# The feed-forward of the latent tokens by seven block products instead of eight, up and down as two phases

## The chip, the core and the metric

The kernel runs on one core of a Trainium2 chip. The metric is the device time of one execution in microseconds (us), as the median of several runs. All data are float32 in DRAM. TensorE gets its dense operands as float32r: each is split into a high part and an exact remainder, and a product costs three passes.

## The reference, cut to what is computed

Two layers share one trunk over 256 context tokens and 1024 latent tokens, with 1024 features. Each layer has a modulated norm, an input projection into four mixers (S5, windowed attention, HGRN2, latent attention), an output projection with a gated residual, and then the part that the change touches, the feed-forward:

```python
def rms_norm(x, g):
    return x * rsqrt(mean(x * x, axis=-1) + EPS) * g
def swiglu(h, w_up, w_down):            # w_up: 1024 x 5632, w_down: 2816 x 1024
    gate, up = split(h @ w_up, 2, axis=-1)
    return (silu(gate) * up) @ w_down
for i in range(2):
    mod = silu_c @ w_mod[i] + b_mod[i]  # 6 * 1024 columns; mod_c likewise for the context
    ...                                 # norm 1, mixers, x = x + g1 * y
    x = x + g2 * swiglu(rms_norm(x, norm2_g[i]) * (1 + sc2) + sh2, ffn_w_up[i], ffn_w_down[i])
    if i == 0:                          # the context as well, with its own modulation
        ctx = ctx + cg2 * swiglu(..., ffn_w_up[i], ffn_w_down[i])
return rms_norm(x, final_norm_g)
```

So the feed-forward of layer 0 covers 1280 tokens and that of layer 1 covers 1024.

## The kernel before

Features lie on the 128 partitions and tokens along them: `x` is a tile of 128 x 8 x 1280. `BLOCKS` cuts the tokens into latent blocks 0 and 1 of 512 and the context block 2 of 256. `H` (class HBuf) holds the scaled input as a high and a low part per block, `Hh` and `Hl`.

**The three passes.** `mm3` (L489 to L494) issues per pair of 128 x 128 weights and a token block three matmuls: high by high, high by low, low by high. `load_split` (L505) loads weights to a staging tile, ScalarE makes the high part (L498) and VectorE, or another engine that is named, the low part (L501).

**The feed-forward.** `ffn` (L1226) goes over the 22 hidden tiles of 128. Per tile it loads two up weights (gate and up, 128 x 8 x 128 each) and one down weight (128 x 1024). `unit_` runs the 24 matmuls of one up product over a token block, then ScalarE's Silu (gate), or VectorE's product with it and a split (up). After two hidden tiles, `down` runs for every block the eight output tiles of these two and adds each to `x` (L1272). So activations never leave SBUF and `x` stays there.

**What runs beside it.** In layer 0 a filler computes layer 1's modulation and S5 matrices. `mod_rows` (L1101) reads a row tile of `w_mod`, and VectorE multiplies it by the condition, once for each of two conditions, with the sum taken on the way (L1116); it yields after each tile, here 96 tiles of 256 KB with two buffers (`modw`), and the condition (`modc`) is loaded per half. Then `s5_build` makes layer 1's matrices in 16 groups; GpSimd (POOL) writes them to DRAM (`s5E`, L312). `paced` (L1727) draws one step of the filler and puts its VectorE work behind what has been traced so far. `ffn` draws a step after each unit and three per block of the down-projection, and what is left before its last tile's end.

**The ends.** `to_next` (L1635) does layer 0's last down-projections block by block: squares, norm 1 of layer 1, loading of the input projection's token weights (`wtmr`, four rounds of 416 KB, then ScalarE and POOL), its first token tiles (`pstm`), then its columns (`psfm`). `to_out` (L1684) does the final norm and the store. The last latent block's norm 2 falls into the first tile of `ffn`, by `start`.

**What sets the order.** The program is traced by a scheduler that gives each engine the ready instruction that stands earliest in the program. A DMA stands in the queue of the engine that issues it (SP's in most cases, POOL's in some) and is held there by its waits. Pools are stacks on the left and the right side of SBUF; a tile that is opened on bytes of an earlier pool waits for that pool's last readers on those bytes.

Of the kernel before, what the change touches and what calls it, by code (L numbers as in the profile page):

```python
# [6 lines left out]
F32 = mybir.dt.float32  # L7
# [9 lines left out]
L = 2  # L17
# [12 lines left out]
# ----------------------------------------------------------------- S5 parameters  # L30
def s5_params(g, raw, keep, big):
    """Powers of a_bar, b_bar, decay and rotation of both layers; layout [(dir, p), layer, group]. raw: lam_re, lam_im, log_dt [128, 3, L * NG]; big: scratch [128, 4096]."""
# [37 lines left out]
    def expm1(x):  # L70
        """(e^x, e^x - 1) to float32 accuracy."""
# [22 lines left out]
    # angle modulo 2 pi, in three parts  # L94
# [27 lines left out]
    # a - 1 without cancellation; b_bar = (a - 1) / lam * B  # L122
# [30 lines left out]
    # powers a^0 .. a^8 : pw[:, re/im, e, (l g)]  # L153
# [10 lines left out]
    # decay over a chunk of 8 and the unit rotation over a chunk  # L164
# [33 lines left out]
def s5_build(g, io, keep, l, gsz, dram, pool, psum, tag):  # L198
# [3 lines left out]
    ls = slice(l * NG, (l + 1) * NG)  # L202
    dsk = g.dsk[:, l]
    # exponents of readout (fwd j+1, bwd 8-j) and drive (fwd 7-j, bwd j)
# [28 lines left out]
    for g0 in range(0, NG, gsz):  # L233
        gs, lg = slice(g0, g0 + gsz), slice(l * NG + g0, l * NG + g0 + gsz)
# [25 lines left out]
        def products(gs=gs, Vm=Vm, R=R, Bz=Bz, Bb=Bb, C=C, nci=nci):  # L260
# [10 lines left out]
            # the products of up to two groups and directions side by side, each on a column tile of its own  # L271
# [19 lines left out]
        # unit rotation e^{i c phi} over the 160 chunks  # L291
# [27 lines left out]
def unit(g, u, ta, tb):  # L319
    """One Newton step to modulus one: u *= 1.5 - 0.5 |u|^2."""  # L320
# [9 lines left out]
def sigmoid(g, out, v, tmp, bias=None):  # L330
    """out = sigmoid(v) by exp and log alone, without overflow."""
# [8 lines left out]
def s5_mixer(g, l, usrc, dram, yraw, last, pool, psum, tag):  # L340
    """usrc: two DRAM [128, T] of the input; yraw: two for the readout. Yields after each part."""
# [107 lines left out]
def s5_glu(g, l, yraw, ydst, blocks, pool, psum, tag):  # L449
    """GELU and GLU of the S5 readout, from DRAM to the high and low parts of the mixers' output. Yields."""  # L450
# [37 lines left out]
def mm3(nc, ps, parts, first=True, last=True):  # L488
    """ps (+)= sum of w^T x over (w_hi, w_lo, x_hi, x_lo) parts, three float32r passes each."""  # L489
    n = len(parts)  # L490
    for i, (wh, wl, xh, xl) in enumerate(parts):
        nc.tensor.matmul(ps, wh, xh, start=first and i == 0, stop=False)  # L492
        nc.tensor.matmul(ps, wh, xl, start=False, stop=False)  # L493
        nc.tensor.matmul(ps, wl, xh, start=False, stop=last and i == n - 1)  # L494
# [9 lines left out]
def load_split(g, pool, shape, src, name, raw, eng=None):  # L504
    """Weights from DRAM as float32r high part and exact remainder; raw: (pool, name) of the staging tile."""  # L505
# [8 lines left out]
# ----------------------------------------------------------------- HGRN2  # L514
# [4 lines left out]
class HGRN:  # L519
    """Gated recurrence of two heads (128 rows) at a time; a token block of one direction after the other, in the order of the scan."""  # L520
# [20 lines left out]
    def unit(self, d, b, z):  # L541
        """z: [128, tn] logits of direction d (PSUM)."""
# [22 lines left out]
        # states and their factors lie value by value; one place more than chunks: the state that enters, whose factor is 0  # L565
# [17 lines left out]
        # keys to token-major, then k^T v of each chunk  # L583
# [14 lines left out]
        # the state leaving a chunk replaces its kv  # L598
# [35 lines left out]
    def finish(self, b, gg, ng, dst):  # L634
        """Head norm and gate gg (PSUM) of one block, to DRAM."""
# [1239 lines left out]
```

## Time and profile before

| | |
|---|---|
| three runs | 3630.08, 3636.73, 3648.10 us; median 3636.73 us |
| the profiled execution: span from first to last instruction | 3633.6 us |
| TensorE (PE) busy | 3460.6 us, 95% |
| VectorE (DVE) busy | 2026.2 us, 56% |
| ScalarE (ACT) busy | 1198.5 us, 33% |
| GpSimd (POOL) busy | 691.0 us, 19% |
| DMA | 280.39 MB, mean 77 GB/s |

Busy times overlap, so they do not add up to the span; an engine that is busy 95% of it has 173 us in which nothing ran on it. PEld is TensorE's loading of weights, which lies beside its matmuls. In rows of the trace, `fpu` is the PSUM bank of an up product, `fpd` of a down product; `out<-in` are names in the program, `x24` is a count, and what stands in brackets is how long the engine had been idle and what it waited for last. One row can stand for several instructions in a row, with their count behind it.

### The profile page before, as it was taken

Reading aid. Unit: us, or ns where it says so; the run is one execution under the profiler, and the core shown is the slowest. Engines: PE = TensorE matmul, PEld = TensorE weight load, DVE = VectorE, ACT = ScalarE, POOL = GpSimd, SP = SyncE. Lnnn points to the kernel's source line nnn. Section 1 sums busy time; section 2 is a strip of 40 time slices with the busy share of each in tenths; the row PEclk is TensorE's granted clock in tenths of the full one; section 3 lists DMA queues with packets and bytes.
Section 4 is the critical chain, followed back from the end, with each engine's and each line's share of the span. In section 5 each row is a group of like instructions: output and inputs, shape, how many; then the busy total and the mean of one; then the engine's idle time right before and its main releaser. Section 6 shows DMA issues by size and latency. Waiting matters only on the chain. (4 is left out here: it accounts for less than half of the span.)

```text
span 3633.6 us, 48522 instructions
## 1 busy us (share of the span) xinstructions
PE 3460.6 (95%) x18654; PEld 2675.0 (74%) x18654; DVE 2026.2 (56%) x4284; ACT 1198.5 (33%) x2120; POOL 691.0 (19%) x1455
## 2 busy tenths in 40 slices
PE   6998998998999999999999998887999999999998
PEld 3877776644678888888888876765644888888887
DVE  7466574568587666555544434564574744334335
ACT  4234444345442111111112435454454521111113
POOL 5730000024320000577100211000045300000000
PEclk8998786899999999999999999786999999999999
DMA  6442213121333333222110332212022311111111
GB/s 207 138 138 95 84 50 99 47 68 40 107 118 112 104 115 105 74 63 59 58 46 18 130 102 88 77 42 58 7 64 71 101 52 47 48 51 47 52 47 58
DMA packets 154503, 280.39 MB, mean 77 GB/s; under 512 B 33344, under 2 KB 81664, under 8 KB 153504
## 3 DMA queue, kind: packets, MB, share of 16 engines
q1 hardware_dynamic: 141120, 260.62, 23.1%
q0 software_dynamic: 3968, 13.77, 1.3%
q10 hardware_dynamic: 9184, 2.91, 0.3%
q8 instruction: 146, 2.39, 0.3%
q14 instruction: 85, 0.70, 0.1%
HBM read 228.14 MB, written 49.09 MB: 76 GB/s over the span
## 5 line engine op out<-in xcount | busy, mean ns | idle before, releaser
L492 PE MATMUL fpu<-Hh,fwh 128*128 128x512 f32 (+1 forms) x1760 | 651.2, 370 | 0.0
L493 PE MATMUL fpu<-Hl,fwh 128*128 128x512 f32 (+1 forms) x1760 | 649.7, 369 | 0.5 <-DVE Hl L1219 0.5
L494 PE MATMUL fpu<-Hh,fwl 128*128 128x512 f32 (+1 forms) x1760 | 648.6, 369 | 0.0
L1272 DVE SCALAR_TENSOR_TENSOR x<-fpd,mod,x 128x512 f32<-128x512 f32 (+1 forms) x448 | 304.9, 686 | 136.6 <-PE fpd L494 134.4
L493 PEld LDWEIGHTS fpu<-Hl,fwh 128*128 128x128 f32 x1760 | 332.2, 189 | 56.8 <-issue 1.2
L492 PEld LDWEIGHTS fpu<-Hh,fwh 128*128 128x128 f32 x1760 | 332.2, 189 | 56.5 <-issue 0.8
L494 PEld LDWEIGHTS fpu<-Hh,fwl 128*128 128x128 f32 x1760 | 332.1, 189 | 56.0 <-DVE fwl L501 0.3
L492 PE MATMUL fpd<-fgh,fdh 128*128 128x512 f32 (+1 forms) x896 | 328.9, 368 | 3.9 <-DVE x L1272 3.3
L493 PE MATMUL fpd<-fgl,fdh 128*128 128x512 f32 (+1 forms) x896 | 327.8, 366 | 0.4 <-DVE fgl L501 0.3
L494 PE MATMUL fpd<-fgh,fdl 128*128 128x512 f32 (+1 forms) x896 | 327.2, 365 | 0.0
L501 DVE TENSOR_TENSOR fwl<-fr,fwh 128x1024 fp32r<-128x1024 f32 x88 | 107.9, 1227 | 305.9 <-ACT fwh L498 304.7
L492 PE MATMUL psfm<-Hh,wfh 128*128 128x512 f32 (+1 forms) x704 | 271.4, 386 | 1.8 <-ACT hgq L539 1.2
L494 PE MATMUL psfm<-Hh,wfl 128*128 128x512 f32 (+1 forms) x704 | 269.3, 383 | 0.0
L493 PE MATMUL psfm<-Hl,wfh 128*128 128x512 f32 (+1 forms) x704 | 266.5, 379 | 0.0
L1116 DVE SCALAR_TENSOR_TENSOR modp<-modw,modc 128x512 f32<-128x512 f32 (+1 forms) x320 | 187.5, 586 | 34.5 <-DMA modw<-in_w_mod 21.8
L1260 DVE TENSOR_TENSOR fsg<-fsg,fpu 128x512 f32<-128x512 f32 (+1 forms) x110 | 69.7, 634 | 239.6 <-PE fpu L494 238.7
L498 ACT CAST fwh<-fr 128x1024 fp32r<-128x1024 f32 x88 | 92.4, 1051 | 329.6 <-PE fpu L493 270.8
L498 ACT CAST fdh<-fr 128x1024 fp32r<-128x1024 f32 x44 | 46.1, 1048 | 446.6 <-PE fpd L493 369.8
L492 PEld LDWEIGHTS fpd<-fgh,fdh 128*128 128x128 f32 x896 | 168.8, 189 | 33.4 <-DVE x L1272 4.9
L493 PEld LDWEIGHTS fpd<-fgl,fdh 128*128 128x128 f32 x896 | 169.1, 189 | 28.3 <-DVE fgl L501 1.2
L494 PEld LDWEIGHTS fpd<-fgh,fdl 128*128 128x128 f32 x896 | 169.1, 189 | 27.1
L1060 POOL TENSOR_TENSOR mlac<-mlac,mlpt 128x1024 f32<-128x1024 f32 x56 | 137.5, 2455 | 113.8 <-ACT mlpt L1023 112.9
(456 smaller groups left out, 6534.1 us busy)
## 6 DMA issues: line engine op xcount, KB each, us to landing
fr<-in_w_up SPq DMA_DIRECT2D x88, 512.0 KB, 3.5
modw<-in_w_mod SPq DMA_DIRECT2D x96, 256.0 KB, 2.7
fr<-in_w_down SPq DMA_DIRECT2D x44, 512.0 KB, 3.5
mw<-in_w_mod SPq DMA_DIRECT2D x32, 512.0 KB, 5.7
wor<-in_w_out SPq DMA_DIRECT2D x32, 512.0 KB, 3.6
wfr<-in_win_fm SPq DMA_DIRECT2D x30, 512.0 KB, 3.5
x<-in_xT SPq DMA_DIRECT2D x4, 2048.0 KB, 18.6
modw<-in_w_mod SPq DMA_DIRECT2D x64, 128.0 KB, 2.5
```

The source lines that it names most:

```text
L492: nc.tensor.matmul(ps, wh, xh, start=first and i == 0, stop=False)
L493: nc.tensor.matmul(ps, wh, xl, start=False, stop=False)
L494: nc.tensor.matmul(ps, wl, xh, start=False, stop=last and i == n - 1)
L498: i = g.nc.scalar.copy(hi, src)
L501: (eng or g.nc.vector).tensor_tensor(out=lo, in0=src, in1=hi.bitcast(F32), op=OP.subtract)
L1060: (V if h == 3 and b > 5 else nc.gpsimd).tensor_tensor(out=acc, in0=acc if b > 1 else prev, in1=pt, op=OP.add)
L1116: V.scalar_tensor_tensor(out=o, in0=w, scalar=1.0, in1=c[:, v], op0=OP.mult, op1=OP.mult, accum_out=part[:, h, t, v:v + 1])
L1260: V.tensor_tensor(out=sl[b], in0=sl[b], in1=ps, op=OP.mult)
L1272: V.scalar_tensor_tensor(out=x[:, m, ts], in0=ps, scalar=g2[:, m, v:v + 1], in1=x[:, m, ts], op0=OP.mult, op1=OP.add)
```

## The change

**Seven products.** With both operands cut into 2 x 2 blocks, a matrix product takes eight block products; a scheme after Strassen (in Winograd's form, with sums that are used again) takes seven, and sums of blocks before and behind. The latent tokens' up and down products are done so. Up: the blocks of a weight tile are gate and up (rows) by the two halves of the features (columns, four tiles of 128 each), and those of the tokens are the halves of the features by token blocks 0 and 1. Down: hidden tiles even and odd, features 0 to 511 and 512 to 1023. Per hidden tile, the latent tokens take 7 x 12 matmuls of 512 columns in place of 96; in down, 7 x 11 x 12 = 924 in place of 1056. The context stays at eight products.

**Up phase** (`Up`). `begin` issues for three tiles the two products that need no sums of tokens. Then `rstd` and `sums`: block 1's values, four combinations of token rows with blocks 0 and 1 on VectorE and POOL, their splits to T6, T7, T4 and into `H`'s own bytes. Then x is freed. `tile` makes four weight sums on POOL (S[0] to S[3]) and runs products 1, 5, 6, 2, (context), 7, 3, 4, (context); two PSUM banks gather them, three snapshots are copied out by ScalarE. Gate times up, in pairs of tiles with four combinations on POOL, goes to DRAM (`gd`, the context's to `gcd`). The filler is drawn twice after each of a tile's yields, from the second tile on (9 yields in layer 0, or 8).

**Down phase** (`Down`). The whole of `w_down` is loaded as raw blocks: A11 to a new pool `da`, the others to `H`'s bytes. x comes back from DRAM (`xm`, stored in the output projection). `run` goes over products 1, 2, 6, 5, 7, 3, 4, each with 11 hidden pairs, four output tiles each; the weights are split, or summed by POOL and VectorE and split, per pair, and the tokens are loaded from `gd` and split. Layer 0 does the context first. Norm 1 of layer 1 for blocks 2 and 1 goes beside product 4.

**Layout.** On the right side x (40 KB per partition in layer 0, 32 in layer 1) is followed in place by pools `fs` (10 KB) and `fg` (21), and beyond them the filler's pools, one after the other (`s5k1` about 11 KB). In the down phase the right edge has `ds` (tiles dh, dl, ds, bt, bh, bl: 36 KB) and next to it `da` (22). The input projection's staging `wtr1` then takes the place of `ds` with one buffer instead of two.

**Filler.** `w_mod1` is cut into quarters of the features instead of halves and its groups are of 8 tiles instead of 48: 192 steps of 128 KB and 24 loads of `modc`. S5's tables are those of layer 1 alone.

```diff
+class Up:
+    def begin(self, j):
+        X, Z = self.bank("fpx"), self.bank("fpz")
+        for ps, h, i in ((X, 0, 1), (Z, 1, 2)):
+            self.product(ps, self.split(self.load(j, 0, h)), i, True)
+        self.begun[j] = X, Z
+    def sums(self, norm, A, sh):
...
+        for k in range(KT):
+            norm.value(k, A, sh)
+        for k in range(4):
+            sub(nc.vector, x0[:, k], xb[:, k], x0[:, k])
+            parts(5, k, x0[:, k])
+        for k in range(4):
+            sub(nc.gpsimd, x0[:, k], xb[:, k + 4], x0[:, k])
+            sub(nc.gpsimd, x0[:, k + 4], x0[:, k + 4], x0[:, k])
+            sub(nc.gpsimd, xb[:, k], xb[:, k + 4], xb[:, k])
+        for i, t, o in ((6, x0, 0), (7, xb, 0), (3, xb, 4), (4, x0, 4)):
+            for k in range(4):
+                parts(i, k, t[:, k + o])
+    def tile(self, j):
...
+        A11, A21, A22, A12 = (self.load(j, s, h) for s, h in ((0, 0), (1, 0), (1, 1), (0, 1)))
+        S = [self.fs.tile([128, 4, 128], F32, name="fs", bufs=5) for _ in range(4)]
+        P.tensor_tensor(out=S[0], in0=A21, in1=A22, op=OP.add)
+        sub(P, S[1], S[0], A11)
+        sub(P, S[2], A11, A21)
+        sub(P, S[3], A12, S[1])
...
+        self.product(X, self.split(S[2]), 7, False)
+        V.tensor_tensor(out=p5, in0=X, in1=p5, op=OP.add)
+        yield
+        self.product(W, self.split(S[3]), 3, False)
+        b = new("fg", 5)
+        V.tensor_tensor(out=b, in0=W, in1=u2, op=OP.add)
+        nc.scalar.activation(out=b, in_=b, func=AF.Silu)
+        V.tensor_tensor(out=b, in0=b, in1=p5, op=OP.mult)
+        yield
+        w22 = self.split(A22)
+        self.product(X, w22, 4, False)
...
+class Down:
+    def split_sum(self, steps):
+        t = self.sp.tile([128, 512], F32, name="ds", bufs=2)
+        for n, (op, a, b) in enumerate(steps):
+            (self.g.nc.vector if n and n == len(steps) - 1 else self.g.nc.gpsimd).tensor_tensor(out=t, in0=t if a is None else a, in1=b, op=op)
+        return self.split_raw(t)
+    def weights(self, i, q):
...
+        if i == 6:
+            return self.split_sum([(OP.add, A[21], A[22]), (OP.subtract, None, A[11])])
...
+        return self.split_sum([(OP.subtract, A[12], A[21]), (OP.subtract, None, A[22]), (OP.add, None, A[11])])
+    def product(self, i, ps, first):
+        for q in range(NQ):
+            w, b = self.weights(i, q), self.tokens(self.gd[i, q], 512)
+            for m in range(4):
+                ms = slice(m * 128, m * 128 + 128)
+                mm3(self.g.nc, ps[m], [(w[0][:, ms], w[1][:, ms], *b)], first and q == 0, i in (2, 3, 4) and q == NQ - 1, i != 2)
+            yield
...
-            with spool("mdc1", LE) as mp:
-                yield from mod_rows(g, 1, io["w_mod1"], 48, mp, 2, slice(0, 48))
+            with spool("mdc1", RI) as mp:
+                yield from mod_rows(g, 1, io["w_mod1"], KT, mp, 2, slice(0, 48))
...
-    o["w_mod1"] = c(f["w_mod"][1].reshape(2, D // 2, 48, 128).transpose(0, 2, 3, 1))
+    o["w_mod1"] = c(f["w_mod"][1].reshape(4, D // 4, 48, 128).transpose(0, 2, 3, 1))
...
+            up = Up(g, l, H, last, TP, wp, pp, gd[l], gcd)
+            for j in range(3):
+                up.begin(j)
+            norms[1].x0 = x[:, :, 0:512]
+            norms[1].rstd(pp, "fx")
+            up.sums(norms[1], sA, sh)
+            RS.release()
+            X.release()
+            with spool(f"fs{l}", RI) as fs, spool(f"fg{l}", RI) as gp:
+                up.open(fs, gp)
+                fill = extra(pp) if l == 0 else iter(())
+                for j in range(NJ):
+                    for _ in up.tile(j):
+                        if j:
+                            paced(g, fill)
+                            paced(g, fill)
+                for _ in fill:
+                    pass
...
+        SL, AP_ = pool(f"ds{l}", RI), pool(f"da{l}", RI)
+        with ppool(f"fq{l}", 8) as pp, spool(f"nf{l}", LE) as npool:
+            dn = Down(g, l, H, x, pp, gd[l], gcd, AP_, SL)
+            for b in bs_out:
+                t0, tn = BLOCKS[b]
+                nc.sync.dma_start(x[:, :, t0:t0 + tn], xm[l][:, :, t0:t0 + tn])
...
+                for i, _ in enumerate(dn.run(lambda b, k: ns[b].square(k))):
+                    if i == 6 * NQ:
+                        save(1)
+                        AP_.release()
+                        AP_ = None
+                        side = early()
...
+                SL.release()
+                ip = InProj(g, 1, pool, RI)
+                ip.start()
+                for i in (8, 9, 4, 5, 6):
+                    ip.tokens(i, H, pp, "fpd", tdst(1))
...
-        self.WR, self.WT = pool(f"wtr{l}", "left", 2), pool(f"wtm{l}", "left")
+        self.WR, self.WT = pool(f"wtr{l}", side, 2 - l), pool(f"wtm{l}", side)
```

## Rows read from the trace of the kernel before

**Rows 1.** Windows: us, busy (count) per engine, PEclk, DMA share, GB/s.

```profile
1083.00:2034.00 951.00, 940.51 (x5006) 802.80 (x5005) 566.50 (x1370) 181.74 (x277) 215.95 (x830) 1.00 0.26 77
2894.00:3620.00 726.00, 724.85 (x3227) 598.51 (x3225) 290.46 (x378) 146.31 (x203) 1.46 (x2) 1.00 0.15 48
3000.00:3200.00 200.00, 200.00 (x883) 165.38 (x882) 74.38 (x92) 32.63 (x43) 0.00 (x0) 1.00 0.15 48
```

**Rows 2.** Timeline of TensorE: start, us, engine, line, operation.

```profile
1083.84 0.28 PE L492 MATMUL fpu<-Hh,fwh 128*128 128x256 f32 x1
...
1951.24 0.28 PE L493 MATMUL fpu<-Hl,fwh 128*128 128x256 f32 x1
1951.36 0.28 PE L494 MATMUL fpu<-Hh,fwl 128*128 128x256 f32 x1
...
2077.35 0.38 PE L492 MATMUL psfm<-Hh,wfh 128*128 128x256 f32 x1 [0.64 <-ACT wtme L1334]
```

**Rows 3.** Timeline at the start of layer 1's feed-forward: the late norm.

```profile
2896.48 0.69 DVE L1197 TENSOR_TENSOR nrs<-nrs,nrq 128x512 f32<-128x512 f32 x1
...
2900.22 1.02 PE L1206 MATMUL nrp<-nrs,ones 128*128 128x512 f32 x2
...
2901.03 1.28 ACT L656 ACT_TABLE_LOAD   x1
...
2904.99 2.07 DVE L1217 SCALAR_TENSOR_TENSOR nru<-x,sA,nrr 128x512 f32<-128x512 f32 x3 [7.06 <-ACT nrr L657]
```

**Rows 4.** Groups of instructions by line and form: busy us, mean ns of one.

```profile
L501 DVE TENSOR_TENSOR fgl<-fsg,fgh 128x512 fp32r<-128x512 f32 x88 | 60.9, 692 | 22.2 <-ACT fgh L498 22.2
...
L498 ACT CAST fgh<-fsg 128x512 fp32r<-128x512 f32 x88 | 54.3, 617 | 124.6 <-DVE fsg L1260 124.2
...
L501 POOL TENSOR_TENSOR Hl<-swy,Hh 128x512 fp32r<-128x512 f32 x8 | 10.8, 1364 | 6.2 <-ACT Hh L498 6.2
```

**Rows 5.** DMA issues (KB each, us to landing); VectorE's timeline in a 128 KB step.

```profile
modw<-in_w_mod SPq DMA_DIRECT2D x64, 128.0 KB, 2.5
...
modc<-scd SPq DMA_DIRECT2D x8, 256.0 KB, 3.6
...
1085.93 0.42 DVE L1116 SCALAR_TENSOR_TENSOR modp<-modw,modc 128x256 f32<-128x256 f32 x1
...
1086.40 0.42 DVE L1116 SCALAR_TENSOR_TENSOR modp<-modw,modc 128x256 f32<-128x256 f32 x1
```

**Rows 6.** POOL's timeline at the S5 tables; tile s5E (first and last start).

```profile
1483.97 0.58 POOL L1632 DMA_DIRECT2D kpw<-kpw  x1 [407.45 <-DVE mod L1121]
...
1503.39 0.09 POOL L294 MEMSET s5E<- 128x1 f32 x1 [1.65 <-DMA s5E<-s5E]
...
L312 POOL DMA_DIRECT2D s5E<-s5E x24: 682/683/697, 54.0 to 1745.0; - x24
```

**Rows 7.** A window at a high DMA rate; DMA issues of the first 50 us.

```profile
935.00:940.00 5.00, 5.00 (x19) 2.14 (x19) 0.69 (x1) 3.90 (x8) 3.00 (x2) 1.00 1.04 387
...
mw<-in_w_mod SPq DMA_DIRECT2D x16, 512.0 KB, 12.0
```

**Rows 8.** Token weights of layer 1's input projection: issues, tile, window of the token tiles.

```profile
wtmr<-in_win_tm SPq DMA_DIRECT2D x8, 416.0 KB, 3.4
...
L498 ACT CAST wtm<-wtmr x8: 868/870/882, 54.4 to 2030.0; 128x832 fp32r<-128x832 f32 x8
...
L501 POOL TENSOR_TENSOR wtm<-wtmr,wtm x4: 1966/2222/2362, 2017.6 to 2031.0; 128x832 fp32r<-128x832 f32 x4
...
2045.00:2077.00 32.00, 31.71 (x169) 31.11 (x167) 10.78 (x16) 12.13 (x20) 2.41 (x1) 1.00 0.21 64
```

**Rows 9.** Timeline: the last down matmul of layer 1.

```profile
3619.78 0.28 PE L494 MATMUL fpd<-fgh,fdl 128*128 128x256 f32 x1
```

**Rows 10.** Timeline of POOL and VectorE near the end of layer 0's output projection.

```profile
1074.11 2.41 POOL L501 TENSOR_TENSOR wol<-wor,woh 128x1024 fp32r<-128x1024 f32 x1 [2.46 <-ACT woh L498]
...
1074.22 2.84 DVE L1217 SCALAR_TENSOR_TENSOR nru<-x,sA,nrr 128x512 f32<-128x512 f32 x1
```

More of the change, by code (lines that the diff above doesn't have):

```diff
@@ L485, in s5_glu, with mm3 @@
             yield
-def mm3(nc, ps, parts, first=True, last=True):
+def mm3(nc, ps, parts, first=True, last=True, read=False):
     n = len(parts)
     for i, (wh, wl, xh, xl) in enumerate(parts):
-        nc.tensor.matmul(ps, wh, xh, start=first and i == 0, stop=False)
-        nc.tensor.matmul(ps, wh, xl, start=False, stop=False)
-        nc.tensor.matmul(ps, wl, xh, start=False, stop=last and i == n - 1)
+        nc.tensor.matmul(ps, wh, xh, start=first and i == 0, stop=False, skip_group_check=read)
+        nc.tensor.matmul(ps, wh, xl, start=False, stop=False, skip_group_check=read)
+        nc.tensor.matmul(ps, wl, xh, start=False, stop=last and i == n - 1, skip_group_check=read)
 def split(g, hi, lo, src, eng=None, pin=False):
@@ L1195, in square @@
             g.nc.tensor.matmul(self.ps[32 * (k % 4):32 * (k % 4) + 32], g.ones[:, 0:32], q, start=k < 4, stop=k >= 4)
-        elif k:
+        elif not first:
             self.eng.tensor_tensor(out=self.s, in0=self.s, in1=q, op=OP.add)
@@ L1562, in hybrid_kernel @@
                 mla.run(LE, others(bs_out[:-1], yp, mpp, "mdp"))
[L1564 to L1565 removed]
+        X, RS = pool(f"x{l + 1}", RI), pool(f"rs{l}", RI)
+        x = X.tile([128, KT, Tn], F32, name="x")
         src = io["xT"] if l == 0 else xs
@@ L1684, in to_out @@
-        def to_out(pp, down, rest, release):
-            def scaled(n, k, eng):
-                o = n.x[:, k]
-                if eng is V:
-                    V.scalar_tensor_tensor(out=o, in0=o, scalar=g.fng[:, k:k + 1], in1=n.rs, op0=OP.mult, op1=OP.mult)
-                else:
-                    eng.tensor_tensor(out=o, in0=o, in1=n.rs, op=OP.mult)
-                if k % 2:
-                    (nc.scalar if k % 4 == 3 and n.t0 == 768 else nc.sync).dma_start(out[k - 1:k + 1, :, n.t0:n.t0 + n.tn].rearrange("k p t -> p k t"), n.x[:, k - 1:k + 1])
-            def block(t0, tn, eng):
-                n = Norm(g, x, t0, tn, npool)
-                def each(k):
-                    n.square(k)
-                    if eng is not V:
-                        nc.scalar.activation(out=n.x[:, k], in_=n.x[:, k], func=AF.Identity, scale=g.fng[:, k:k + 1])
-                down(t0, tn, each)
-                if t0 < 768:
-                    table_set("natural_log_exp_and_others")
-                n.rstd(pp, "fx")
-                return n
-            with spool("nf", RI, 2) as npool:
-                n = block(0, 512, V)
-                for i, _ in enumerate(rest):
-                    for k in range(4 * i, 4 * i + 4):
-                        scaled(n, k, V)
-                release()
-                for t0, eng in ((512, nc.gpsimd), (768, V)):
-                    n = block(t0, 256, eng)
-                    for k in range(KT):
-                        scaled(n, k, eng)
@@ L1716, in hybrid_kernel, with extra @@
-        ffn(g, l, x, H, bs_out, start, to_out if last else to_next, extra if l == 0 else None)
+        def extra(pp):
+            with spool("mdc1", RI) as mp:
+                yield from mod_rows(g, 1, io["w_mod1"], KT, mp, 2, slice(0, 48))
+            with spool("s5k1", RI) as kp:
+                keep = {"pw": kp.tile([128, 2, 9, NG], F32, name="kpw"), "lad": kp.tile([128, 8, 2, NG], F32, name="klad"),
+                        "f": kp.tile([128, 2, NG], F32, name="kf")}
+                for n in keep:
+                    nc.gpsimd.dma_start(keep[n], keepd[n][..., NG:])
+                yield from s5_build(g, io, keep, 1, 1, dram, kp, pp, "fx", NG)
@@ new lines, in hybrid_kernel @@
+        TP, wp = pool(f"ft{l}", LE), pool(f"fw{l}", LE)
+        H.new((1,))
+        with ppool(f"fp{l}", 1) as pp:
+            up = Up(g, l, H, last, TP, wp, pp, gd[l], gcd)
[16 more added lines that the diff above has]
+                    pass
```

411 lines of the change are left out of this document (263 added, 148 removed).

## Prediction

> **What bounds the kernel now.** I read the page's busy row and its forty slices first: TensorE is busy 95% of the span, no other engine above 56%. The windows come next [rows 1]: in both feed-forwards TensorE is busy for nearly the whole window (940.5 of 951 us in layer 0, 724.9 of 726 us in layer 1), at full granted clock, with VectorE at 60% and 40% and the DMA engines at a quarter or less. Busy time counts each matmul with its pipeline, so the price of a matmul is the distance between two starts: 883 in 200 us for 128x512, 0.2265 us each [rows 1], and 0.12 us for 128x256 [rows 2]. By those prices the feed-forward is at its floor: 3168 large matmuls are 717.6 us, all of layer 1's window but 8 us. So only fewer matmuls can help, and everything that the change lays between them costs in full.
>
> The profiled execution has a span of 3633.6 us; the three runs lie from 3630.1 to 3648.1 with a median of 3636.7, so I add my sum to the median and count 3 us for what lies around the span. I call the first feed-forward matmul of a layer t = 0; in layer 0 that is 1083.84, and layer 1's column projections begin at 2077.35, t = 993.5 [rows 2].
>
> **What goes.** A hidden tile's latent tokens took 96 matmuls of 512 columns and take 84; down, 1056 become 924. That is 264 + 132 = 396 fewer per layer, 89.7 us a layer, 179.4 us in all. Context work is unchanged. No rival questions this term: the code issues fewer.
>
> **Start of the up phase, both layers.** `begin` gives TensorE 72 matmuls, 16.3 us. Then it needs the sums. In the trace the norm's sum was ready at 2897.17, but its matmul ran at 2900.22, behind the 24 matmuls that stand ahead of it in the program [rows 3]. `rstd` stands behind `begin`, so I let it run at 16.3. From there to the first scaled row took 4.8 us, with two table loads [rows 3]. `sums` then needs: eight values on VectorE at 2.07 / 3 us, 5.5 [rows 3]; difference, cast, low part of the first row, 2.0; twelve POOL differences at 1.36, 16.4; the last row's cast and low part, 1.3 [rows 4]. Only then is x free, and x lies on the bytes of pool `fs`, where the weight sums go: one more POOL sum and a cast, 2.0. TensorE restarts at 16.3 + 4.8 + 27.2 = 48.3 and has idled 31 us. If the norm's matmul slips in as soon as it is ready (3 us after t = 0) it is 18; if VectorE and POOL take turns, 41. I take 31, the order that the row shows.
>
> **Filler in layer 0's up phase.** This is the step that decides. Modulation and S5 matrices must be done before `da` can be loaded: `ds` fills the right edge to 36 KB, `da` lies at 36 to 58; in the up phase `fs` and `fg` take 31 KB and the filler's `s5k1` lies at 31 to 42. The modulation is now 192 steps of 128 KB with two buffers, and 24 reloads of `modc` with one. A step is two VectorE instructions of 0.47 (1085.93 to 1086.40), 0.93; a load lands in 2.5, `modc` in 3.6 [rows 5]. A buffer thus turns in 3.5, two of them give a step every 1.75; eight steps are 12.3 us, then 3.65 for `modc`: 16 us a group, 24 groups 384. VectorE's other work lengthens it; I take 16.5, 396 (bounds 15 and 18.5: 360 and 444). The pace laid out in the code is no help: 17 steps are laid out per tile of 24.8 us, 1.46 us a step, faster than the loads turn. A step that waits for its load also holds what is queued behind it on VectorE (low parts of weights, X + P5), and TensorE waits for those, but that only moves idle time forward.
>
> The S5 build can't start sooner: in the trace its tables waited for the modulation's last instruction, since they lie on its bytes, and then POOL took 16.1 us a group until 1745.0, 16 groups, 258 us, about 3.3 us after the tables were asked for [rows 6]. POOL's weight sums of the last tiles fit into the gaps of 1.65 us between groups; I add 5 (bound 38).
>
> So: tile 0 ends at 48.3 + 60 x 0.2265 + 48 x 0.12 = 67.6, where the filler starts. Modulation ends at 464, S5 at 464 + 3.3 + 258 + 5 = 730. TensorE's own up work ends at 48.3 + 529 = 577 at the earliest. It then waits for the first piece of A11: load and cast, 5 us: 735.
>
> **Down phase.** Context 528 x 0.12 = 63.4, seven products 924 x 0.2265 = 209.3, both layers alike but for the context. In layer 0 the loads are hidden in the wait. In layer 1 they are not: the other weight blocks (8.6 MB) and x (4.2 MB) become loadable only as the last products finish, 12.9 MB at 387 GB/s is 33 us from 8 us before the end on [rows 7], and the tokens go through the same SP queue behind them; a 512 KB load that stood in such a queue landed in 12.0 us [rows 7]. I take 18 idle us, between 8 (tokens first) and 25 (tokens last). Products 3 and 6 need POOL sums, two and one of 1.36 per block of 2.72 us: 5 us a layer, between 0 and 31 (below). Additions to x hide beside the next product.
>
> **End of layer 0.** `wtr1` has one buffer and lies on `ds`, so four rounds of load 3.4, cast 0.87, POOL 2.2 follow the last matmul one by one, 26 us [rows 8]; one token tile ends 1.5 later and nine follow at 24 x 0.19: 69 us to the column projections, half of it idle. Before, this loading lay beside the last down-projections.
>
> **End of layer 1.** Before, 13.8 us from the last matmul to the end of the span [rows 9]. After: addition, square, norm, eight rows of 512 over two engines, one DMA; I come to the same within 2 us: 0. Stores of x and activations: hidden, DMA share stays under a half. Snapshots that TensorE waits for in the first tiles, and slower first matmuls after an idle stretch: 3 us in layer 0 and 6 in layer 1, an estimate.
>
> **Sum.** Layer 0: 735 + 63.4 + 209.3 + 5 + 69 + 3 = 1085, against 993.5: +91. Layer 1: -89.7 + 31 + 18 + 5 + 6 = -30. Together +61: **3698 us**. Its own bounds: all small ends give layer 0 +25 and layer 1 -61, 3601; all large ones would pass 3800; its own range is 3640 to 3765.
>
> **Port.** A row bears on the sums: at 1074.11 POOL began an instruction of 2.41 us, and VectorE's, with two inputs from SBUF, took 2.84 instead of 0.74 [rows 10].
> The Trainium skill ("SBUF — State Buffer", Who interferes with whom) says why: a VectorE instruction with two SBUF inputs and a POOL one that reads SBUF exclude each other for their whole length. The trace agrees by those two rows. By that rule POOL and VectorE times add up wherever both are needed, which is rival 2.
>
> **Rivals.** (1) The filler is hidden; the other side. If loads turn faster than I reckon, or S5 does not wait, up ends at 577, and 18 + 63.4 + 209.3 + 5 + 69 give 942, some 8 more for S5's own matmuls: 950, -44; with layer 1 -74: **3563**. For it: the pace as laid out ends in tile 18. Against: two buffers, and 16.1 us a group on POOL whatever the pace. It decides from a filler end before t = 590. (2) POOL and VectorE take turns. Product 3 needs 2 x 1.36 + 3 x 0.69 = 4.8 us per block instead of 2.72, product 6 3.4: 31 us a layer instead of 5, and 10 more at each start: +72, **3770**. For it [rows 10]; against: in layer 0's window POOL was busy 216 us beside VectorE, and TensorE lost under 11 of 951 [rows 1]. (3) The matmuls that go come back as waits inside the up phase, in the 2.7 us between product 7 and product 4; some 0.3 us a tile, 13 us; inside the range.
>
> **Chances.** Forecast 0.55, hidden filler (1) 0.28, taking turns (2) 0.14, waits that alone bring no gain (3) 0.03. About 0.5% (18 us) is what a measurement here can tell from no change. Faster: most of the second, a twentieth of the first: 0.28. Same: 0.09. Slower: 0.63. The range reaches from the hidden filler with one small end more to rival 2: 3545 to 3770.
>
> **What would show it.** Layer 0: TensorE idle for over 100 us between its last up and first down matmul, ended by the `da` load, with POOL's s5E work running until then; modulation ending near t = 460 and s5E near 730; TensorE idle some 30 us before the fourth S product's first use in both layers, 10 to 25 us before layer 1's first down matmul, some 25 us before the first pstm. Wrong if s5E ends before the up phase does, or if the span falls by more than 30 us.

## The result, and the profile after

The changed kernel takes 3978.5 us (median of four runs, 3970.5 to 3985.3) against 3633.6 before: 1.096 times as long, 95% interval 1.092 to 1.100. The forecast was 3698, range to 3770. The profiled execution has a span of 3968.7 us, 335 more than before. Split at TensorE's own landmarks (first up matmul of a layer, first `psfm` of layer 1):

| stretch | before | after | difference | forecast |
|---|---|---|---|---|
| start to layer 0's feed-forward | 1083.8 | 1072.3 | -11.5 | 0 |
| layer 0's feed-forward to the column projections | 993.5 | 1274.9 | +281 | +91 |
| layer 1's mixers, to its feed-forward | 817.4 | 884.6 | +67 | 0 |
| layer 1's feed-forward to the end | 738.8 | 736.9 | -2 | -30 |

The first row mixes two things. Up to the output projection TensorE and VectorE have the same order of instructions in both programs; the changed one got there 21 us earlier (939.0 instead of 959.9), with a granted clock of 0.82 from 400 to 600 and 0.87 from 600 to 800, where the kernel before had 0.77 and 0.82. From there to the first up matmul it took 133 us instead of 124: the change costs some 9 us there, in no term of the forecast. In all runs this stretch is 133 to 136 us with the changed layer 0 and 124 with that of before. TensorE's longest waits in it are 4.2 us for a cast of the projection's weights, whose casts begin at 936.5 instead of 887.4 and whose loads now stand behind the stores of x (`xm`) in SP's queue, and 4.1 us for the norm's sum ahead of `begin`. What each part costs was not tried.

First the page's busy row of after. Then windows of after, in the columns of [rows 1]: layer 0's up phase, the wait before its down phase, that phase; layer 1's mixers; layer 1's up phase, wait and down phase. Last, the window of layer 1's mixers in the kernel before.

```profile
PE 3358.9 (85%) x17812; PEld 2558.8 (64%) x17812; DVE 2353.9 (59%) x5001; ACT 1637.8 (41%) x2878; POOL 1270.6 (32%) x1841
```

```profile
1072.00:1929.00 857.00, 610.83 (x3130) 506.19 (x3128) 546.45 (x1585) 198.42 (x361) 395.74 (x960) 0.86 0.34 105
1929.00:1971.00 42.00, 0.01 (x1) 0.01 (x1) 5.15 (x8) 4.13 (x7) 6.17 (x5) 0.55 1.00 358
1971.00:2275.00 304.00, 285.77 (x1456) 240.54 (x1456) 215.35 (x343) 151.95 (x284) 85.48 (x53) 0.98 0.34 96
...
2347.00:3232.00 885.00, 785.99 (x4329) 550.66 (x4329) 457.35 (x783) 504.09 (x802) 174.95 (x104) 0.86 0.21 68
3232.00:3680.00 448.00, 423.82 (x1849) 348.19 (x1848) 250.71 (x296) 177.91 (x298) 208.37 (x142) 0.97 0.31 102
3680.00:3718.00 38.00, 0.21 (x1) 0.21 (x1) 5.08 (x7) 2.50 (x5) 5.58 (x5) 0.56 1.01 368
3718.00:3950.00 232.00, 218.97 (x925) 175.03 (x926) 152.24 (x216) 98.14 (x171) 85.35 (x53) 0.98 0.32 92
```

```profile
2077.00:2895.00 818.00, 754.24 (x4327) 531.51 (x4328) 458.62 (x782) 383.37 (x702) 178.50 (x105) 0.90 0.23 72
```

Over the span TensorE is busy 102 us less, but in layer 0's up phase it is busy for only 611 of 857 us. The mixers, whose matmuls did not change, show ScalarE with 100 instructions and 121 us more.

What TensorE waited for in layer 0's up phase (`fpx` and `fpw` are banks of its products, `s5tp` is a transpose in the S5 build), and below it what SP's queue and VectorE waited for in the S5 stretch (1620 to 1912): engine, line, releaser, us in total, times, longest.

```profile
PE s5tp L266 <- DVE s5V L224: 120.7, 10, 42.5
PE fpx L492 <- DVE fsn L1367: 65.0, 16, 7.1
PE s5tp L266 <- DVE s5t L242: 35.6, 3, 34.4
PE fpw L492 <- ACT fh L498: 22.6, 1, 22.6
```

```profile
SPq L1395 <- POOL s5Et L310: 42.9, 1, 42.9
SPq L1393 <- POOL s5E L306: 37.0, 1, 37.0
SPq L1393 <- POOL s5Et L310: 35.6, 1, 35.6
SPq L1395 <- POOL s5E L308: 31.1, 1, 31.1
...
DVE s5nci L247 <- DMA s5C<-in_s_c: 146.5, 6, 42.9
```

The two fences are one chain. Its links in the first of four such stalls (31 to 43 us, 142 in all), from the timeline:

```profile
1661.61 0.39 PE L493 MATMUL fpx<-Tl,fh 128*128 128x512 f32 x1
...
1683.68 1.26 POOL L1247 TENSOR_TENSOR fgt<-fg,fgt 128x512 f32<-128x512 f32 x1
...
1684.97 0.32 SPq L1395 DMA_DIRECT2D gd<-fgt  x1
...
1687.23 0.55 SPq L237 DMA_DIRECT2D s5C<-in_s_c  x1
...
1689.50 0.17 DVE L247 TENSOR_SCALAR s5nci<-s5C 128x16 f32<-128x16 f32 x1 [30.88 <-DMA s5C<-in_s_c]
...
1692.78 0.45 PE L266 MATMUL s5tp<-ident,s5V 128*128 128x128 f32 x1 [30.78 <-DVE s5V L224]
```

POOL does the sum of a pair of tiles behind S5's E work; SP's queue stands at the store of that sum; S5's next table stands behind the store; VectorE, and everything laid behind it, waits for the table; TensorE stands at S5's transpose, with the up products behind it.

### The profile page after: what moved, and what is told of

Same layout as the page of the kernel before. It is cut to its first block, busy times and chain, and to the rows that moved or that the text cites. A ratio compares the mean times of both kernels' runs of the same rounds, so it can differ in the third digit from the quotient of the medians.

```text
span 3968.7 us, 51362 instructions
## 1 busy us (share of the span) xinstructions
PE 3358.9 (85%) x17812; PEld 2558.8 (64%) x17812; DVE 2353.9 (59%) x5001; ACT 1637.8 (41%) x2878; POOL 1270.6 (32%) x1841
## 5 line engine op out<-in xcount | busy, mean ns | idle before, releaser
L492 PE MATMUL fpd<-bh,dh 128*128 128x512 f32 (+1 forms) x792 | 290.7, 372 | 81.3 <-ACT bh L498 80.7
L1116 DVE SCALAR_TENSOR_TENSOR modp<-modw,modc 128x256 f32<-128x256 f32 x512 | 275.9, 539 | 121.9 <-DMA modc<-scd 66.7
L493 PE MATMUL fpd<-bl,dh 128*128 128x512 f32 (+1 forms) x792 | 297.0, 375 | 27.5 <-DVE bl L501 27.2
L494 PE MATMUL fpd<-bh,dl 128*128 128x512 f32 (+1 forms) x792 | 293.5, 371 | 2.8 <-DVE dl L501 2.8
L492 PE MATMUL fpx<-Th,fh 128*128 128x512 f32 x528 | 217.7, 412 | 65.2 <-DVE fsn L1367 65.0
L492 PEld LDWEIGHTS fpd<-bh,dh 128*128 128x128 f32 x792 | 151.8, 192 | 109.0 <-ACT bh L498 82.7
L494 PE MATMUL fpx<-Th,fl 128*128 128x512 f32 x528 | 214.8, 407 | 0.0
L493 PE MATMUL fpx<-Tl,fh 128*128 128x512 f32 x528 | 214.4, 406 | 0.0
L493 PEld LDWEIGHTS fpd<-bl,dh 128*128 128x128 f32 x792 | 151.9, 192 | 63.6 <-DVE bl L501 39.5
L494 PEld LDWEIGHTS fpd<-bh,dl 128*128 128x128 f32 x792 | 152.0, 192 | 28.3 <-DVE dl L501 4.6
```

What stands on the lines that cost most here:

```text
L493: nc.tensor.matmul(ps, wh, xl, start=False, stop=False, skip_group_check=read)
L1116: V.scalar_tensor_tensor(out=o, in0=w, scalar=1.0, in1=c[:, v], op0=OP.mult, op1=OP.mult, accum_out=part[:, h, t, v:v + 1])
```

## The experiments

A ratio is to the kernel before, with its 95% interval; medians of 4 runs at least.

**1. ScalarE's tables.** In the trace of after, ScalarE loads 111 tables of 1.28 us; before, 16. Where the first of them lie (timeline of ScalarE):

```profile
1919.90 1.28 ACT L1559 ACT_TABLE_LOAD   x1
...
1929.22 1.28 ACT L1372 ACT_TABLE_LOAD   x1 [7.66 <-DMA s5R<-s5KD]
1930.51 0.63 ACT L1372 ACTIVATE fg<-fg 128x512 f32<-128x512 f32 x1
...
2424.48 1.28 ACT L656 ACT_TABLE_LOAD   x1
2425.78 0.47 ACT L656 ACTIVATE acsq<-acps,eps 128x256 f32<-128x256 f32 x1
2426.27 1.28 ACT L657 ACT_TABLE_LOAD   x1
2427.56 0.42 ACT L657 ACTIVATE acsq<-acsq 128x256 f32<-128x256 f32 x1
```

The preload of the set that serves both logarithm (L656) and exponential (L657) came 9 us before the last Silu (L1372), which loaded its own set over it. The preload is pinned behind the ScalarE instruction traced last, a cast of weights that is ready early, not behind the Silu. From then on each of the two functions loads a set of its own.

```diff
-        nc.scalar.activation(out=b, in_=b, func=AF.Silu)
+        self.silu = nc.scalar.activation(out=b, in_=b, func=AF.Silu).ins
...
-            table_set("natural_log_exp_and_others")
+            with tc.issue_after(up.silu):
+                nc.scalar.preload_act_table_set("natural_log_exp_and_others")
```

> The changed kernel, with the ScalarE table preload of the down phase queued behind the last Silu of the up phase instead of behind the instruction traced last. Theory (the preload ran ahead of the last Silu, whose own load threw it out again, so that from there on every logarithm and every exponential loads its own table: 111 loads of 1.28 us against 16 before): loads fall to about 20, layer 1's mixers (column projections to the first feed-forward matmul) from 885 us to about 820, the whole by 55 to 75 us. Rival (the mixers are slower for another reason, their order or a lower clock by chance): the loads fall, the time by less than 15 us.

Measured: 3912.1 us, 1.077 (1.073 to 1.081), 66 us less; 5 loads; mixers 832 us. The same stretch:

```profile
1932.49 0.63 ACT L1372 ACTIVATE fg<-fg 128x512 f32<-128x512 f32 x1 [7.72 <-DMA s5R<-s5KD]
1933.13 1.28 ACT L1865 ACT_TABLE_LOAD   x1
...
2423.92 0.48 ACT L656 ACTIVATE acsq<-acps,eps 128x256 f32<-128x256 f32 x1
2424.43 0.42 ACT L657 ACTIVATE acsq<-acsq 128x256 f32<-128x256 f32 x1
```

The Trainium skill ("ScalarE: Activation LUTs", Table sets: the hidden batching unit) says that a logarithm and then an exponential need one load where the set with both is active. The trace agrees: none stands between 2423.92 and 2424.43, and one stands ahead of each function where the set was lost.

**2. The same in the kernel before.** One `table_set` line (L1679) is taken out.

> The kernel before, with one line taken out: the table preload ahead of layer 0's last norm, the last one before layer 1's mixers. Nothing else of the change is in it. Theory of the tables: some 80 loads appear in layer 1's mixers, which go from 817 to 870-890 us, the whole 45 to 75 us slower. Rival: within 15 us of the kernel before.

Measured: 3697.2 us, 1.015 (1.011 to 1.019), 62 us more; 109 loads; mixers 886 us. So the tables are nearly the whole of the +67, shown from both sides; without their loads, layer 1's mixers took 817 to 834 us in all runs. Some 5 us of the rest lie, as in layer 0, between the first matmul of the output projection and the first up matmul: 98 us instead of 93.

**3 and 4. No filler.** `extra` becomes a copy, in the changed kernel and in the one before; layer 1's modulation and S5 matrices are left out:

```diff
+            V.tensor_copy(out=g.mod[:, 1], in_=g.mod[:, 0])
+            for n in "RVE":
+                dram[n][1] = dram[n][0]
```

> The changed kernel without the filler: layer 1's modulation and S5 matrices are left out (layer 0's are read in their place). Theory (the filler sets the end of layer 0's up phase, and the waits of TensorE inside it are the filler's): the up phase falls from 856 to about 585 us (545 of matmuls, 23 at its start, some small waits), the whole by 250 to 280 us. Rival (the up phase waits for itself: the sum with product 5 between products 7 and 4, weight sums on POOL): some 65 us of short waits stay, the up phase stays above 630, the whole falls by less than 225 us.

> The kernel before without the filler (layer 1's modulation and S5 matrices left out in the same way). Both theories: the filler was hidden there, TensorE idled 9 us in the whole feed-forward of layer 0, and S5's own matmuls are some 8 us; so 0 to 20 us less than the kernel before. If it falls by more than 40, the filler cost time before as well and experiment 3 overstates what the change made of it.

Measured: 3704.4 us, 1.019 (1.016 to 1.022), 274 less than the changed kernel; and 3613.0 us, 0.993 (0.990 to 0.996), 22 less than before. The up phase takes 574 us, its window:

```profile
1087.60:1661.60 574.00, 551.31 (x2904) 476.13 (x2904) 257.17 (x352) 200.06 (x346) 216.14 (x144) 0.98 0.25 88
```

No wait above 0.8 us is left in it but the one at its start: the short waits were the filler's too. The forecast had this end at 577. With 22 us of filler in the kernel before, the change made it dearer by 252.

**5 to 7. Pace and cut of the filler.** Experiment 5 adds an empty step behind each S5 step; experiment 6 cuts the modulation as before; 7 does both.

```diff
-                yield from mod_rows(g, 1, io["w_mod1"], KT, mp, 2, slice(0, 48))
+                yield from mod_rows(g, 1, io["w_mod1"], 48, mp, 2, slice(0, 48))
...
-    o["w_mod1"] = c(f["w_mod"][1].reshape(4, D // 4, 48, 128).transpose(0, 2, 3, 1))
+    o["w_mod1"] = c(f["w_mod"][1].reshape(2, D // 2, 48, 128).transpose(0, 2, 3, 1))
```

> The changed kernel with the S5 steps of the filler drawn half as often (each followed by an empty step). Theory A (the filler's own length sets the end: POOL has 258 us of S5 work to do behind the modulation, whenever the steps are drawn): the four stalls of 31 to 43 us go, but TensorE then waits at the end for what is left; S5 ends within 15 us of t = 830, the time falls by 0 to 25 us. Rival B (the stalls themselves are the loss: steps drawn faster than POOL can do them hold SP's queue, VectorE and TensorE): the time falls by 100 to 150 us.

> The changed kernel with the modulation cut as before: 96 steps of 256 KB in one group and 2 loads of modc, in place of 192 of 128 KB in 24 groups. Theory: a step is two instructions of 0.85 us on VectorE and a buffer turns in 2.7 + 1.7 us, so 2.2 us a step, 211 us in all; modulation ends near t = 300 instead of 548. S5 then ends near t = 590, but its steps still come faster than POOL can do them, so some 140 us of stalls stay inside the up phase: it falls from 856 to 730-770, the whole by 85 to 130 us. If the filler's end alone counts (no loss by the stalls), the up phase falls to 600-620, the whole by 230 to 260. Rival (small steps and reloads of modc cost nothing, VectorE's share sets the modulation's length): less than 30 us.

> Experiments 5 and 6 in one: modulation cut as before, S5 steps drawn half as often. Theory: S5's 97 steps at 8.5 a tile of 24.8 us are as slow as POOL's 258 us, so nothing stalls, and the filler ends at t = 590 to 640, about with the up phase: it falls from 856 to 590-640, the whole by 210 to 265 us. If the filler is bound by VectorE or POOL in another way, the up phase stays above 700.

Measured: 3894.4 (1.074), 3927.6 (1.082) and 3933.6 us (1.084). Experiment 5 has 10 table loads (in its order the preload happened to come after the Silu): its layer-1 mixers are 62 us shorter for that, layer 0's feed-forward only 18, and S5 ends at t = 825: theory A in the end and the time, but not in the stalls, of which four of 26 to 39 us stayed. Experiment 6 shows the cut's price: modulation ends at t = 335 instead of 548. But only 43 us of the 213 reached the end of the feed-forward, fewer than I expected: the four stalls stay (29 to 38 us each), and the up phase, which can't use them, becomes 812. And 7 missed: drawn half as often, the stalls are nearly the same (26 to 38 us), and POOL's E work ends at t = 622 instead of 618. `paced` lays only VectorE's part of a step behind what is traced; the E work on POOL depends on nothing but tables and runs ahead whenever it is drawn.

**8. Load order.** Ahead of the first tokens only A11 is asked for; the rest follows between the token loads.

```diff
+                    if name == 11:
+                        go()
+                    else:
+                        self.later.append(go)
...
             w, b = self.weights(i, q), self.tokens(self.gd[i, q], 512)
+            self.ask(2)
```

> The changed kernel with the order of the down phase's loads turned: only A11 is asked for ahead of the first tokens; the other three weight blocks and x follow between the token loads of the first product (layer 1) or of the context (layer 0). Theory (the first tokens stand behind 13 MB in SP's queue, which is the 42 and 38 us that TensorE idles before the first down matmul): both gaps fall to 8-15 us, and with the slower clock behind them the whole falls by 50 to 75 us. Rival (A11's own 2.9 MB and the landing of gd's last stores set the gap): gaps stay above 30, less than 15 us.

SP's queue before the first down matmul of layer 1 in the changed kernel, and that matmul:

```profile
3683.57 3.29 SPq L1419 DMA_DIRECT2D da<-in_w_down  x6
3686.90 10.21 SPq L1419 DMA_DIRECT2D mw<-in_w_down  x10
3698.13 3.61 SPq L1863 DMA_DIRECT2D x<-xm  x2
3701.78 18.38 SPq L1450 DMA_DIRECT2D bt<-gd  x7
```

```profile
3717.79 0.80 PE L492 MATMUL fpd<-bh,dh 128*128 128x512 f32 x1 [37.98 <-ACT bh L498]
...
3719.96 0.63 PE L493 MATMUL fpd<-bl,dh 128*128 128x512 f32 x1
3720.39 0.63 PE L494 MATMUL fpd<-bh,dl 128*128 128x512 f32 x1
```

The tokens are asked for at 3701.78, 18 us behind the first weights. Measured: 3937.0 us (1.086), 41 less, of which 34 lie in the two feed-forwards; the gaps fall from 42 and 38 us to 19 and 16. Less than expected: the products beside which the loads now run became longer (the context in layer 0 from 66 to 77 us, the first product in layer 1 from 32 to 40).

**9 and 10. POOL's queue.** Experiment 9 moves the four pair sums to VectorE; 10 moves S5's E work there instead (`W = nc.vector` for layer 1).

> The changed kernel with the four sums of a pair of tiles on VectorE instead of POOL. In the changed kernel's S5 stretch SP stands 147 us in four waits for these sums, which lie on POOL behind S5's E work; S5's next tables stand behind them on SP, VectorE waits 147 us for the tables, TensorE behind VectorE. Theory (POOL's 258 us of E work set the length anyway; SP is only the way in which that reaches TensorE): SP's four waits go, S5 still ends near t = 820-835, the time falls by 0 to 30 us. Rival (SP's queue is the cause): the stalls go, and the time falls by 90 to 150 us.

> The changed kernel with layer 1's S5 E work on VectorE instead of POOL (its store goes through SP). Theory (the E work on POOL is what makes S5 280 us long and puts POOL's sums, SP, VectorE and TensorE behind it): no stall over 15 us stays in the S5 stretch, S5 takes 130 to 190 us instead of 280, the up phase falls from 856 to 690-760 and the whole by 95 to 160 us. Rival (VectorE becomes the queue in which everything stands, its instructions being laid between TensorE's own): up phase above 800, less than 50 us.

Measured: 3916.0 (1.079) and 3886.7 us (1.072). Experiment 9 lies between theory and rival: the long stalls go and the up phase falls from 856 to 783 us, but S5 still ends at t = 808, and TensorE waits 59 us for it and for the loads; 62 us in all. The first down matmul comes at t = 842 instead of 899, 56 us earlier, but 27 of these lie in the modulation, which ended at t = 522: so at most some 30 of the 147 us in SP's waits were a loss; the rest is POOL's work, which had to be waited for in any case. In experiment 10 no stall over 9 us stays in the up phase but the one at its start, yet VectorE needs 240 us for S5, and TensorE waits at the end again (first down matmul at t = 808): 92 us, just under what was expected.

**11 to 13. Causes together.** 11 is 6 and 10; 12 adds 1 and 8; 13 also draws the modulation half as often.

> Experiments 6 and 10 in one: modulation in 96 steps as before, E work on VectorE. Theory: modulation ends near t = 338 as in experiment 6, S5 near t = 500, before the up phase's own end; what stays is some 50 us of short waits beside the modulation: up phase 630-680 (574 without filler), the whole 170 to 225 us faster than the changed kernel, 3755 to 3810. If the up phase stays above 720, VectorE is short.

> Experiment 11 with the table preload of experiment 1 and the load order of experiment 8. If the causes add up: 3755-3810 less 62-66 for the tables less 35-45 for the loads, 3645 to 3710, so still 0.3% to 2% slower than the kernel before: what stays is 2 x 23 us at the start of the up phases, short waits beside the modulation, the token weights at the end of layer 0. Faster than before only if the short waits go too.

> Experiment 12 with the modulation's steps drawn half as often: 8.5 a tile of 24.8 us, 2.9 us a step, slower than a buffer turns (2.2). Theory (a step that waits for its load holds VectorE, the sum of product 7 with product 5 stands behind it, TensorE waits for that sum): the waits of 2 to 6 us before product 4 go (some 45 us, and 10 to 15 of slower clock behind them), modulation ends near t = 355 instead of 339; the up phase falls from 723 to 660-690, the whole by 35 to 60 us against experiment 12, to 3675-3700. Rival (VectorE is simply full beside the modulation): less than 15 us.

Measured: 3843.7 (1.059), 3733.5 (1.030; 1.026 to 1.033) and 3710.4 us (1.021; 1.018 to 1.025). 11 and 12 miss by 34 and 24 us: the up phase stays at 724 and 722, with VectorE's filler steps in TensorE's way until S5 ends at t = 634; behind that TensorE waits for nothing. 13 comes just short of its theory: up phase 693, 30 us less by the ratios; the waits for the sum with product 5 shrink from 35 us (in 12) to 24 and do not vanish. So loads that are waited for are a part of it. VectorE's plain load is probably another (it is busy 521 of the 578 us beside the filler in 11); no run parts the two further. With a filler, layer 0 stays behind the kernel before: 1089 us against 993.5.

**14. POOL out of two places**, on the base of 12.

```diff
-            sub(nc.gpsimd, x0[:, k], xb[:, k + 4], x0[:, k])
+            sub(nc.vector, x0[:, k], xb[:, k + 4], x0[:, k])
...
+            P.tensor_tensor(out=A[12], in0=A[12], in1=A[11], op=OP.add)
...
+            P.tensor_tensor(out=A[12], in0=A[12], in1=A[21], op=OP.subtract)
...
-        return self.split_sum([(OP.subtract, A[12], A[21]), (OP.subtract, None, A[22]), (OP.add, None, A[11])])
+        return self.split_sum([(OP.subtract, A[12], A[22])])
```

> Experiment 12 with POOL out of two places: the twelve differences of tokens at the start of the up phases go to VectorE, and product 3's weight sum, three sums in a row, is spread over products 5, 7 and 3 (A12 is turned into A12 + A11, then - A21, in place). Theory (POOL's 1.3 us and VectorE's 0.7 us sums take turns, so POOL's help costs more than the work on VectorE alone): the idle of 23 us after begin falls to 14-18 in both layers, product 3 from 45.7 to 31-35 us in both, products 5 and 7 gain at most 3 us: the whole 25 to 45 us less than experiment 12, 3690 to 3710. Rival (POOL works beside VectorE): the start grows longer by the work moved (some 8 us), product 3 stays above 40, no gain.

In 12, the twelve differences on POOL at the start of layer 1's up phase, a VectorE instruction with two inputs from SBUF beside them (1.76 us; such a difference takes 0.69 alone, [rows 4]), and the window of product 3:

```profile
3018.12 20.33 POOL L1247 TENSOR_TENSOR x<-x 128x512 f32<-128x512 f32 x12 [22.39 <-DVE x L1247]
...
3024.21 1.76 DVE L1247 TENSOR_TENSOR x<-x 128x512 f32<-128x512 f32 x1
```

```profile
3634.55:3680.30 45.75, 34.08 (x134) 25.15 (x132) 33.45 (x43) 15.34 (x28) 26.53 (x18) 0.96 0.24 69
```

Measured: 3719.7 us, 1.022 (1.017 to 1.027), by the ratios 27 us less than 12; the intervals of the two just meet, but the two feed-forwards in the profiles are 11 and 16 us shorter. The idle at the start falls from 22 to 17 us in both layers, though VectorE does all the work; product 3 from 45.7 to 30.5. Products 2 and 6 took 4 us longer each in both layers. The window of product 3 in 14:

```profile
3647.60:3678.05 30.45, 30.21 (x134) 24.70 (x133) 22.72 (x30) 14.76 (x26) 11.69 (x8) 1.00 0.31 96
```

Product 2 in layer 1, in 12 and then in 14:

```profile
3510.90:3540.80 29.90, 29.90 (x133) 24.77 (x132) 17.00 (x27) 12.86 (x23) 2.59 (x2) 1.00 0.33 97
...
3515.70:3549.60 33.90, 31.84 (x134) 24.21 (x133) 33.90 (x25) 12.56 (x22) 31.89 (x20) 1.00 0.26 78
```

The sums in place, written into products 5 and 7, depend on nothing but the weights: POOL ran both ahead, in product 2 (32 of 34 us busy, 20 sums). VectorE's work there, 17 us in 12, then filled all 34. So POOL's sums did not go away, they took turns with VectorE in another product.

**15 and 16. Layer 1 alone.** Layer 0 is that of before; 16 has the mends of 1, 8 (one load per step, x in pieces) and 14.

> The kernel before with the change in layer 1 alone; layer 0's feed-forward, its filler and its ends are those of before. Theory (the costs in layer 1 are its own: 23 us of idle at the start, 38 before the first down matmul, 23 in the down phase, so of 90 us some 2 are left): layer 1's feed-forward to the end takes 732 to 740 us (739 before, 737 in the changed kernel), its mixers 815 to 835, the whole within 15 us of the kernel before.

> Experiment 15 with what was found: table preload behind the last Silu, only A11 ahead of the first tokens (the other blocks and x, in pieces, one load per step), differences on VectorE, product 3's sum spread. If these add up: 38 us before the first down matmul become 16, 23 at the start become 16, product 3 loses 13, a little clock: layer 1's feed-forward to the end takes 685 to 705 us, the whole 25 to 50 us less than the kernel before, 3585 to 3610.

Measured: 3646.5 us, 1.002 (1.000 to 1.005), no difference; and 3603.8 us, 0.992 (0.989 to 0.995), 0.8% faster than the kernel before and the fastest of all. Its windows of up phase, wait and down phase:

```profile
2896.00:3337.00 441.00, 423.94 (x1849) 348.19 (x1848) 247.50 (x308) 175.16 (x295) 188.72 (x130) 0.98 0.30 104
3337.00:3353.00 16.00, 0.44 (x1) 0.29 (x1) 2.95 (x5) 2.77 (x5) 3.08 (x3) 0.60 0.98 355
3353.00:3582.00 229.00, 219.23 (x926) 176.05 (x925) 166.63 (x208) 96.49 (x170) 108.78 (x66) 0.98 0.40 131
```

From the first up matmul to the end it takes 702 us against 739: of 90 us of matmuls 37 reach the end.

## Why the prediction was wrong

- **What goes** held: 179 us of matmuls. Without filler and tables the change would stand near 3704 - 66 = 3638 us, beside 3613 for the kernel before without filler (an estimate from experiments 3 and 1, which were not run together): even there its own waits eat the whole gain.
- **Start of the up phase**: forecast 31 us of idle, measured 22.6 and 23.8. The norm's matmul did not stand behind `begin` (it ran before it), and POOL and VectorE did take turns: both alternatives named beside the forecast, 13 us less and 10 more, held at once. The 4 us of waiting for the norm's sum then lie ahead of `begin`, where no term had them.
- **Filler** was the deciding step. That its end holds back the down phase was right; its sizes failed, and so did the reading that its waits cost nothing inside the up phase. First down matmul: t = 735 forecast, 899 measured. The last modulation steps and the last table store in the changed kernel, with t = 0 at 1072.3 (first and last start):

```profile
L1116 DVE SCALAR_TENSOR_TENSOR modp<-modw,modc x512: 397/424/2622, 259.8 to 1620.2; 128x256 f32<-128x256 f32 x171
...
L312 POOL DMA_DIRECT2D s5E<-s5E x24: 682/682/697, 51.2 to 1901.3; - x24
```

  The difference of 164 us has four terms, of some 84, 16, 26 and 37. Modulation ended at t = 548, not 464: a group took 20.5 us, not 16.5, since a buffer's next load was asked for only after VectorE had come to it between the up phase's own instructions (SP waited 146 us for that). S5's E work ended at 830, 16 us more than forecast: POOL was busy 216 us from 1621 to 1902, against 197 in the same work before. The last up matmul came 26 us behind it, because stalls had held TensorE back; "that only moves idle time forward" was wrong by that much here, and by much more once the filler is shorter (experiment 6). And 42 us, not 5, lie between the last up and first down matmul: "in layer 0 the loads are hidden in the wait" failed, since the up phase ended behind the filler and the places come free only with it, as in layer 1 (in experiment 10 it ended 77 us ahead of S5, and 12 us were left behind S5). By the prediction's own sign the step failed too: s5E ended 26 us before the up phase did, and in place of over 100 us of idle behind the last up matmul stand 42 us there and 142 in the four stalls inside the phase.
- How a wait for `modc` reaches TensorE, in the timelines of VectorE and TensorE of the changed kernel (L1367 is the sum with product 5):

```profile
1478.41 0.43 DVE L1116 SCALAR_TENSOR_TENSOR modp<-modw,modc 128x256 f32<-128x256 f32 x1 [2.92 <-DMA modc<-scd]
...
1483.51 0.69 DVE L1367 TENSOR_TENSOR fsn<-fpx,fsn 128x512 f32<-128x512 f32 x1
...
1484.25 0.79 PE L492 MATMUL fpx<-Th,fh 128*128 128x512 f32 x1 [7.09 <-DVE fsn L1367]
```

- **Tables**: no term of the sum had them; 62 to 66 us. [Rows 3] showed a load of 1.28 us between the norm's matmul and its scaling (the trace has a second one at 2903.03, ahead of the exponential), and I priced them as a fixed part of the start; what they tell is which set was active. The diff moves the preloads, and I did not ask what each stands behind.
- **Down phase**: forecast 214 us for the seven products, measured 233 in layer 1 (239 in layer 0, where norm work slows product 4). Product 3 alone lost 16 us: rival (2) at that one place, with 4.2 us a block where the rival had 4.8 and the forecast 2.7. The Trainium skill's rule on the shared port ("SBUF — State Buffer", Who interferes with whom), by which a VectorE instruction with two inputs from SBUF contends with one of POOL that reads SBUF, should have had more weight: experiment 14 gains where it takes work from POOL (45.7 to 30.5 us) and loses where POOL's sums come to lie (29.9 to 33.9).
- **Wait before layer 1's down phase**: 38 us, not 18. The bound of 25 (tokens last) left out that a token load waits in the same queue for all that was asked before.
- **End of layer 0**: 72 us, forecast 69. **End of layer 1**: 18 us from the last matmul, forecast 14.
- Rival (1), a hidden filler, fell: it would have needed an end before t = 590. Rival (3) was there (65 us of short waits), but as a part of the filler's price.

## What to carry to other kernels

A filler that fits beside a long phase has to be priced again when the phase gets shorter or its engines busier: by the engine that does it, and by every queue in which its steps stand ahead of the main work. After a change that moves activations, count the table loads: a preload must be queued behind the last function of the old set, not behind whatever was traced last. And POOL was no help where VectorE was needed at the same time: in experiment 14 the start and product 3 became shorter without its sums, and product 2 longer with them.

## What the runs showed of the hardware

- A table load took 1.283 us each time and began as the instruction before it ended (2424.48 after a copy until 2424.47), with the activation 0.02 us behind it. The Trainium skill ("ScalarE: Activation LUTs", What ACT_TABLE_LOAD costs) gives 1283 ns, which agrees, and 1380 ns of drain besides, which these rows do not show. 93 to 106 loads cost 62 to 66 us of the whole.
- After 38 us of idle, TensorE's matmuls of 512 columns started 0.43 us apart instead of 0.2265 until 3722, 4 us: the granted clock was at its half level (1.2 of 2.4 GHz) from 3684 on. In the up phase of layer 0 the lower level lay on 79 us of busy time, half of it lost.
